# A decoder step with fp32 products from three passes: new orders and engine lists for the attention, the heads and the output projection

## The chip, the core and the metric

The kernel runs on one core of one Trainium2 chip. The core has a matmul engine (PE, with its weight loads shown as PEld), three engines for elementwise work (DVE, ACT and POOL) and SP, which here issues DMAs. The metric is the device time of one execution in microseconds (us), taken as the median of several runs; lower is better.

## The reference

It is one inference step of two layers over 512 prompt tokens and 8 single new tokens (520 columns together), width 1024, all in fp32. Layer 0 is native sparse attention with a paged cache, layer 1 an mLSTM with four heads of 512. Cut to what matters:

```python
x = x + (attend(rmsnorm(x) @ w_in) * silu(z)) @ w_out           # layer 0
# attend: gates[0]*compressed + gates[1]*selected + gates[2]*window, each a masked softmax over its keys
h = rmsnorm(x)                                                   # layer 1
xm, zm = split(h @ m_w_in)
c = silu(conv4(xm));  q, k, v = block4(c), block4(c), block4(xm)
C = decay * C + k (w v)^T                                        # 8 samples: state 4 x 512 x 512 each
S = (q k^T) * exp(D - m)                                         # prompt: one causal matrix for each head
hc = (S v) / max(|sum S|, exp(-m))                               # samples: q C + ... instead of S v
out = (hc * rsqrt(mean(hc^2)) * norm_w + skip * c) * silu(zm)
x = x + out @ m_w_out
y = rmsnorm(x)
```

The outputs are y, the new cache rows, and the new states C, n, m and conv.

## The kernel before

**Products.** An fp32 product is made of three fast passes. Every operand is split into a high part (`whi`, `hhi`, `uh`, `vh`, `kwh`, `Sh`) and the rest (`wlo`, `hlo`, `ul`, `vl`, `kwl`, `Sl`); `mm3` adds hi x hi, hi x lo and lo x hi in PSUM. A high part is a copy (by ACT or DVE), a low part a subtraction (by DVE or POOL). Some products run as plain fp32 (`s<-q,CT`, `mm<-CT,bdm`, `t<-bdk,ctw`), and those with the samples' state (`d<-cs,QZ`) use 32 columns of the array at a time, four side by side.

**Stages.** In time order: the input side of layer 0 (projection, compressed keys), the attention, then output projection, norm and the projection to xm with its convolution, then the gate side zm, then the heads of the mLSTM with most of its output projection, then a tail with the last head's output and the final norm. One weight tile passes through `wraw` (from HBM), `whi` and `wlo`.

**Order.** The program's text is not issued as it stands. Two recorders hold it back and replay it in an order written out by hand as a table of numbers. `Plan` holds named operations (a piece of work on one engine with what it reads and writes) and replays them at `P.run(ORDER0, R, NE, MOVEDP0)` (L1625, the attention), `P.run(ORDER1, ...)` (L2308, zm) and `P.run(ORDER2, R, NE, MOVEDP2)` (L2705, the heads). `Rec` holds every single instruction and replays at `R.run(NE, CALLS0, ...)` (L1024), `CALLS2` (L1415), `CALLS1, MOVED1` (L1952: output projection, norm, xm) and `CALLS3` (L2756, the tail). Each engine runs its own queue strictly in the order of issue; between engines semaphores hold back what needs another's result or buffer. Buffers come from pools that go round in the order of issue.

A number that also stands in a `MOVED` list changes engine when it is replayed:

```python
def swapped(engines, e, m, a, k):                        # L478
    if m == "activation":                                # a copy by ACT goes to DVE
        engines["DVE"].tensor_copy(a[0], a[1])
    elif m == "tensor_copy" and e == "DVE":              # a copy by DVE goes to ACT
        engines["ACT"].activation(a[0], a[1], AF.Copy)
    else:                                                # sub, mul, add, scalar: DVE <-> POOL
        getattr(engines["POOL" if e == "DVE" else "DVE"], m)(*a, **k)
```

Since every instruction goes through `Engine.__getattr__.call` (L504), all records of the profile bear this one line, and operations are told apart by the names of their tiles.

**The heads.** For each head and each of its four blocks of 128 columns `qk` (L2339) does: `mm<-CT,bdm` (PE) and its copy `q`; `ctw` (DVE), `t<-bdk,ctw` (PE), `kwh` (a copy) and `kwl` (a subtraction) of it; `s<-q,CT` (PE), the scores; and twelve `mm<-vh,kwh`, `mm<-vl,kwh`, `mm<-vh,kwl`, the new state C of the prompt, copied out by `cpt`. `values` (L2440) multiplies scores by decays (`wt`), splits them into `Sh` and `Sl`, and forms `num`; `sq` and `acc` are squares and their sum for the norm; `hx` and `hy` the factor; then num x `hy`, + `CT`, x `zs`, and the split into `uh` and `ul`. `out_unit` (L2633) is one tile of the output projection: `wraw`, `whi`, `wlo`, `mm<-uh,whi` and so on, and `x` += `mm`. For the samples `state_step` (L2014) does one of 32 pairs of head and sample: the state `cs` in, `d<-cs,QZ` (PE; `QZ` is q with the other samples at zero), `t<-VB,OH` (PE, v spread over the partitions), `cs` scaled (ACT), `cs` += `t` x `wk` (DVE), and `cs` out. In the attention, `pt` is a copy of softmax weights, `dxo` and `dPS` belong to the samples, and `mn` is the softmax maximum.

Of the kernel before, what the change touches and what calls it, by code (L numbers as in the profile page):

```python
# [540 lines left out]
def step_kernel(ctx, tc, ap):  # L541
# [1082 lines left out]
    P.LAT, P.SELF = 0.24, 0.07  # L1624
    P.run(ORDER0, R, NE, MOVEDP0)  # L1625
    actx.close()
# [324 lines left out]
    xm_val(15)  # L1951
    R.run(NE, CALLS1, MOVED1)  # L1952
    mctx.close()
# [912 lines left out]
```

## Time and profile before

| | |
|---|---|
| median of 3 runs | 1042.33 us (1041.23 to 1043.42) |
| the profiled execution | 1037.7 us, span 1036.0 us, granted clock 0.998 |
| PE busy | 1012.9 us, 98% of the span |
| PEld | 909.0 us, 88% |
| DVE | 784.4 us, 76% |
| ACT | 532.7 us, 51% |
| POOL | 380.6 us, 37% |
| memory | read 145.89 MB, written 58.10 MB, 197 GB/s over the span |

The busy time of PE is that of records whose ends are modelled; matmuls overlap, so consecutive starts are closer than the records are long. In the rows of the timeline the first number is the start in us, the second the length; square brackets hold the engine's idle time before the row and who ended it; `x8` are that many instructions grouped.

### The profile page before, as it was taken

To read this page: it belongs to the slowest core of one execution; us is meant where nothing else is said; L and a number is where in the kernel's file an instruction comes from. 1 tells how busy PE (TensorE), PEld (TensorE's weight loads), DVE (VectorE), ACT (ScalarE), POOL (GpSimd) and SP (SyncE) were. 2 spreads that over 40 slices of the span, in tenths; PEclk is the share of its full clock that TensorE was granted. 3 is DMA by queue.
4 is the path that set the end of the run, shared out by engine and by line. 5 is a ranking of instruction groups with operands and counts; after the bars stand their busy time and mean duration, and the time that the engine had idled before them with its cause. 6 is when DMAs were issued, how large, how long until landed. Compare 5 with 4: busy or idle time off the path is not lost.

```text
span 1036.0 us, 24026 instructions
## 1 busy us (share of the span) xinstructions
PE 1012.9 (98%) x8743; PEld 909.0 (88%) x8743; DVE 784.4 (76%) x1879; ACT 532.7 (51%) x1228; POOL 380.6 (37%) x430
## 2 busy tenths in 40 slices
PE   7999999999999999999999999999999999999998
PEld 6989999899998888779999998898857678877987
DVE  7876764568568987775887786866677888989885
ACT  5253342533268877761444455656655665463543
POOL 1072433301246656362234433332323335434330
PEclk9999999999999999999999999999999999999999
DMA  7664453133335624547434642688789789898543
GB/s 251 200 199 143 152 163 121 50 117 118 113 100 159 188 84 123 164 144 255 144 110 166 209 144 73 245 277 304 276 269 358 256 273 316 284 338 287 190 137 113
DMA packets 124793, 197.19 MB, mean 190 GB/s; under 512 B 16118, under 2 KB 66167, under 8 KB 124419
## 3 DMA queue, kind: packets, MB, share of 16 engines
q1 hardware_dynamic: 118866, 186.37, 54.7%
q10 hardware_dynamic: 5808, 9.28, 2.5%
q8 instruction: 69, 1.13, 0.4%
q14 instruction: 50, 0.40, 0.1%
HBM read 145.89 MB, written 58.10 MB: 197 GB/s over the span
## 4 chain that ended last, share of the span: by engine, by line
PE 67%; DVE 5%; ACT 2%; POOL 1%; issue 0%; DMA 0%; ACTq 0%; DVEq 0%
PE mm L504 44%; PE s L504 9%; PE t L504 8%; PE d L504 6%; ACT s L504 1%; DVE num L504 1%; DVE s L504 1%; POOL s L504 0%; DMA wraw<-in_m_in 0%; DVE ul L504 0%; DVE x L504 0%; ACT pt L504 0%; DVE wlo L504 0%; DVE hx L504 0%; DVE sc L504 0%
## 5 line engine op out<-in xcount | busy, mean ns | idle before, releaser
L504 PE MATMUL mm<-hhi,whi 128*128 128x260 f32 (+1 forms) x952 | 273.1, 287 | 0.9 <-ACT hhi L504 0.9
L504 PE MATMUL mm<-hhi,wlo 128*128 128x260 f32 (+1 forms) x952 | 269.9, 283 | 2.1 <-POOL wlo L504 1.1
L504 PE MATMUL mm<-hlo,whi 128*128 128x260 f32 (+1 forms) x952 | 269.6, 283 | 0.0
L504 PEld LDWEIGHTS mm<-hhi,whi 128*128 128x128 f32 (+1 forms) x952 | 178.4, 187 | 5.6 <-issue 3.6
L504 PEld LDWEIGHTS mm<-hhi,wlo 128*128 128x128 f32 (+1 forms) x952 | 178.3, 187 | 2.8 <-DVE wlo L504 1.5
L504 PEld LDWEIGHTS mm<-hlo,whi 128*128 128x128 f32 (+1 forms) x952 | 178.1, 187 | 0.8 <-DVE hlo L504 0.2
L504 POOL TENSOR_TENSOR wlo<-wraw,whi 128x1024 fp32r<-128x1024 f32 (+2 forms) x49 | 94.5, 1931 | 177.1 <-DVE whi L504 118.1
L504 DVE SCALAR_TENSOR_TENSOR cs<-t,wk,cs 128x512 f32<-128x512 f32 x128 | 89.1, 743 | 13.0 <-ACT cs L504 11.3
L504 ACT ACTIVATE cs<-cs,SBC 128x1024 f32<-128x1024 f32 x64 | 71.6, 1144 | 33.8 <-PE d L504 31.2
L504 POOL TENSOR_SCALAR s<-s,sm 128x256 f32<-128x256 f32 (+3 forms) x69 | 70.1, 1026 | 38.6 <-DVE sm L504 20.2
L504 ACT ACTIVATE s<-s,mn 128x256 f32<-128x256 f32 (+3 forms) x128 | 70.6, 554 | 16.8 <-DVE mn L504 12.8
L504 PE MATMUL s<-phi,w1h 128*128 128x256 f32 (+1 forms) x256 | 77.1, 301 | 0.0
L504 PE MATMUL s<-plo,w1h 128*128 128x256 f32 (+1 forms) x256 | 74.7, 292 | 2.3 <-DVE plo L504 2.3
L504 PE MATMUL s<-phi,w1l 128*128 128x256 f32 (+1 forms) x256 | 74.1, 289 | 0.0
L504 DVE TENSOR_TENSOR wlo<-wraw,whi 128x1024 fp32r<-128x1024 f32 (+1 forms) x53 | 61.1, 1154 | 9.2 <-ACT whi L504 4.5
L504 ACT ACTIVATE whi<-wraw 128x1024 fp32r<-128x1024 f32 (+1 forms) x53 | 46.7, 884 | 38.8 <-DMA wraw<-in_m_out 14.1
L504 PE MATMUL mm<-uh,whi 128*128 128x260 f32 x224 | 65.1, 291 | 0.0
L504 PE MATMUL mm<-uh,wlo 128*128 128x260 f32 x224 | 63.3, 282 | 1.5 <-DVE wlo L504 1.5
L504 DVE CUSTOM_DVE_ANT_0 s<-s,D 128x512 f32<-128x512 f32 (+3 forms) x128 | 57.8, 488 | 7.8 <-PE s L504 7.4
L504 PE MATMUL mm<-ul,whi 128*128 128x260 f32 x224 | 63.2, 282 | 0.0
L504 PEld LDWEIGHTS s<-plo,w1h 128*128 128x128 f32 x256 | 48.4, 189 | 4.0 <-DVE plo L504 2.8
L504 PEld LDWEIGHTS s<-phi,w1h 128*128 128x128 f32 x256 | 48.3, 189 | 0.6
(481 smaller groups left out, 2623.4 us busy)
## 6 DMA issues: line engine op xcount, KB each, us to landing
cs<-in_state_C SPq DMA_DIRECT2D x64, 512.0 KB, 6.5
o_cs<-cs SPq DMA_DIRECT2D x64, 512.0 KB, 5.0
praw<-in_cache SPq DMA_DIRECT2D x128, 128.0 KB, 3.0
dk<-in_cache SPq DMA_DIRECT2D x128, 128.0 KB, 2.6
wraw<-in_m_in SPq DMA_DIRECT2D x32, 512.0 KB, 4.0
wraw<-in_m_out SPq DMA_DIRECT2D x32, 256.0 KB, 4.9
wraw<-in_w_kv SPq DMA_DIRECT2D x11, 512.0 KB, 3.7
wraw<-in_w_q SPq DMA_DIRECT2D x8, 512.0 KB, 3.8
```

Source lines behind the costliest of these rows:

```text
L504: return f(*[real(x) for x in a], **{n: real(x) for n, x in k.items()})
```

## The change

Three tables of order are stated anew: `ORDER0` (934 numbers), `ORDER2` (933) and `CALLS1` (712); each is a permutation of the same numbers, with nearly all at another place (in the mean 10, 15 and 24 places away, at most 106, 135 and 251). With them go the lists of what changes engine: `MOVEDP0` from 118 to 123 numbers (41 new, 36 gone), `MOVED1` from 139 to 136 (62 new, 65 gone), `MOVEDP2` from 116 to 94 (44 new, 66 gone). `ORDER1`, `CALLS0`, `CALLS2`, `CALLS3` and their lists, all pools and all functions stay. PE and SP get the same instructions in another order; DVE has 20 instructions fewer, in the attention 392 and then 391, in the projection 268 and 245, in the heads 445 and 449 (ACT 244 and 247, 176 and 185, 230 and 239; POOL 104 and 102, 80 and 94, 101 and 88).

```diff
 ORDER0 = (
-    828, 792, 54, 55, 57, 834, 830, 8, 9, 108, 10, 11, 13, 14, 12, 71, 15, 37, 28, 793, 16, 17, 59, 60, 34, 61,
+    911, 830, 828, 792, 54, 55, 8, 13, 9, 10, 834, 11, 12, 71, 14, 15, 16, 17, 37, 28, 31, 61, 59, 57, 793, 18,
...
-MOVEDP2 = (82, 94, 170, 177, 189, 265, 272, 284, 285, 286, 288, 292, 295, 309, 338, 346, 357, 362, 373, 387, 388, 389,
+MOVEDP2 = (75, 82, 265, 285, 301, 304, 309, 328, 331, 347, 352, 356, 357, 373, 377, 387, 388, 391, 396, 397, 400, 405,
```

DVE at the start of the heads. `HN` is the last piece of the sample gates, `VT` is v of the prompt, `QKS` q and k of the samples, `pr`, `wk` and `nT` small parts of the samples' state n. Before:

```order
L504 TENSOR_TENSOR HN<-nm,dn 128x32
L504 CAST vh<-VT_9863 128x512
L504 CAST vh<-VT_10476 128x512
L504 COPY QZ_10218<-QKS 128x8 x4
L504 COPY q<-mm 128x512
L504 TENSOR_TENSOR pr<-QKS 128x32
L504 TENSOR_TENSOR pr<-QKS,nT 128x32
L504 TENSOR_TENSOR wk<-QKS,SBC 128x32
```

After:

```order
L503 TENSOR_TENSOR HN<-nm,dn 128x32
L503 COPY QZ_9877<-QKS 128x8 x4
L503 TENSOR_TENSOR VB<-t,VB 8x512
L503 ISA ctw,cwn<-CT_9724,wb 128x512
L503 ISA cwn 128x1
L503 ISA ctw,cwn<-CT_9799,wb 128x512
```

The copies `QZ` now follow `HN` directly; the two casts `vh` and the copy `q` are no longer on this engine here, and the small parts come behind `VB` and two `ctw`.

PE at the start of the heads, from the first `t<-bdk,ctw` to the first product with `kwh`. Before:

```order
L504 MATMUL t<-bdk,ctw 128x128 x4
L504 MATMUL s<-q,CT_9898 128x512
L504 MATMUL s<-q,CT_9898 128x384
L504 MATMUL s<-q,CT_9898 128x256
L504 MATMUL s<-q,CT_9898 128x128
L504 MATMUL mm<-CT_10067,bdm 128x512
L504 MATMUL t<-bdk,ctw 128x128 x4
L504 MATMUL s<-q,CT_9950 128x512
L504 MATMUL s<-q,CT_9950 128x384
L504 MATMUL s<-q,CT_9950 128x256
L504 MATMUL s<-q,CT_9950 128x128
L504 MATMUL mm<-vh,kwh 128x512
```

After:

```order
L503 MATMUL t<-bdk,ctw 128x128 x4
L503 MATMUL mm<-CT_10034,bdm 128x512
L503 MATMUL t<-bdk,ctw 128x128 x4
L503 MATMUL t<-VB,OH 128x512
L503 MATMUL mm<-vh,kwh 128x512
L503 MATMUL mm<-vl,kwh 128x512
```

The two blocks of scores that stood between `t<-bdk,ctw` and the product now stand ahead of both.

DVE at the end of the heads, up to the last `wlo` of the stage. Before:

```order
L504 TENSOR_TENSOR x_13343<-x_13343,mm 128x260 x2
L504 TENSOR_TENSOR x_12924<-x_12924,mm 128x260
L504 TENSOR_TENSOR num<-num,hy 128x512
L504 SCALAR_TENSOR_TENSOR num<-CT_11135,par,num 128x512
L504 TENSOR_TENSOR num<-num,zs 128x512 x2
L504 TENSOR_TENSOR wlo<-wraw,whi 128x512
```

After:

```order
L503 TENSOR_TENSOR x_12816<-x_12816,mm 128x260
L503 TENSOR_TENSOR x_13200<-x_13200,mm 128x260 x2
L503 TENSOR_TENSOR num<-num,hy 128x512
L503 SCALAR_TENSOR_TENSOR num<-CT_11127,par,num 128x512
L503 TENSOR_TENSOR num<-num,zs 128x512 x2
L503 TENSOR_TENSOR wlo<-wraw,whi 128x512
```

The `wlo` stands behind the same operations on `num`; from `hx` to it there are six additions to `x`, where there were seven.

More of the change, by code (lines that the diff above doesn't have):

```diff
@@ L251 @@
 CALLS1 = (
[33 rows of a table removed]
-)
-MOVED1 = (20, 27, 29, 30, 36, 45, 52, 61, 62, 69, 71, 72, 73, 79, 88, 89, 95, 104, 112, 117, 126, 127, 152, 157, 164,
[6 rows of a table removed]
[33 rows of a table added]
+)
+MOVED1 = (27, 29, 30, 36, 45, 46, 59, 67, 68, 72, 73, 79, 88, 89, 95, 105, 117, 124, 126, 127, 147, 152, 157, 164,
[6 rows of a table added]
 MOVED2 = (8, 9, 28, 47, 66, 84, 103, 104, 122, 123, 141, 142, 161, 177, 179, 185, 210, 212, 227, 240, 242, 249, 268,
@@ L295 @@
 MOVED3 = (2, 12, 16, 23, 30, 31, 35, 42, 65, 69, 103, 120, 124, 136, 141,)
-MOVEDP0 = (19, 20, 23, 24, 41, 47, 64, 65, 66, 67, 69, 84, 93, 95, 99, 119, 120, 123, 164, 166, 167, 184, 186, 190,
[5 rows of a table removed]
+MOVEDP0 = (7, 19, 20, 23, 24, 41, 47, 50, 64, 66, 69, 84, 86, 89, 93, 95, 98, 99, 119, 120, 124, 164, 167, 184, 186,
[5 rows of a table added]
 MOVEDP1 = (7, 27, 31, 42, 46, 47, 61, 77, 82, 87, 91, 112, 117, 127, 132, 136, 162, 166, 167, 172, 177, 181, 182, 192,
     196, 197, 202, 211, 212, 248, 255,)
-MOVEDP2 = (82, 94, 170, 177, 189, 265, 272, 284, 285, 286, 288, 292, 295, 309, 338, 346, 357, 362, 373, 387, 388, 389,
[5 rows of a table removed]
+MOVEDP2 = (75, 82, 265, 285, 301, 304, 309, 328, 331, 347, 352, 356, 357, 373, 377, 387, 388, 391, 396, 397, 400, 405,
[4 rows of a table added]
 LATE = ((3, 1), (3, 2), (3, 3))
```

269 rows, old and new, of tables (CALLS1, MOVED1, MOVEDP0, MOVEDP2) are left out of this document.

## The prediction

> **What bounds the kernel now.** I read the page's head first, then the windows, one for each stage, then the waits inside the three stages that are stated anew, and the timeline at the longest waits.
>
> ```profile
> PE 1012.9 (98%) x8743; PEld 909.0 (88%) x8743; DVE 784.4 (76%) x1879; ACT 532.7 (51%) x1228; POOL 380.6 (37%) x430
> ```
>
> The matmul engine is busy for 98% of the span, so time can come only from its 23.1 us of idle, from waits too short to show as idle, and from the cost of its own order. The windows say where the idle lies. Their columns are the stretch, its length, and each engine's busy time; the stretches are the input side, the attention, the output projection with norm and xm, zm, the heads, and the tail.
>
> ```profile
> core 0: us, PE busy (x) PEld busy (x) DVE busy (x) ACT busy (x) POOL busy (x), PEclk, DMA share, GB/s
> 0.00:307.00 307.00, 294.00 (x2431) 286.98 (x2431) 208.33 (x428) 124.03 (x301) 90.47 (x95) 1.00 0.45 144
> 307.00:467.00 160.00, 159.01 (x1902) 132.19 (x1899) 131.81 (x517) 122.00 (x377) 92.14 (x107) 0.99 0.48 143
> 467.00:647.00 180.00, 179.81 (x1572) 175.91 (x1576) 133.36 (x277) 77.05 (x176) 64.57 (x80) 1.00 0.47 157
> 647.00:751.00 104.00, 101.70 (x858) 92.72 (x851) 73.77 (x134) 62.61 (x119) 33.23 (x40) 1.00 0.79 276
> 751.00:993.00 242.00, 239.74 (x1725) 186.03 (x1724) 208.63 (x457) 129.78 (x215) 90.38 (x101) 1.00 0.83 282
> 993.00:1036.00 43.00, 38.61 (x269) 35.14 (x268) 28.54 (x70) 17.20 (x40) 9.77 (x9) 1.00 0.34 111
> ```
>
> Length less PE busy gives 13.0, 1.0, 0.2, 2.3, 2.3 and 4.4 us. The three stages that change (second, third and fifth row) hold 1.0 + 0.2 + 2.3 = 3.4 us of idle in 582 us; the other 19.7 us lie where the order stays. The granted clock is 0.99 to 1.00, so no stage is slowed by it. The waits of PE, in these three windows in turn (total, times, longest):
>
> ```profile
> PE t L504 <- DVE dxo L504: 0.2, 1, 0.2
> PE t L504 <- ACT pt L504: 0.2, 1, 0.2
> PE s L504 <- DVE mn L504: 0.2, 1, 0.2
> PE d L504 <- ACT pt L504: 0.2, 1, 0.2
> ...
> PE t L504 <- DVE sr L504: 0.2, 1, 0.2
> ...
> PE mm L504 <- DVE wlo L504: 1.5, 1, 1.5
> PE d L504 <- DVE QZ L504: 0.4, 1, 0.4
> PE mm L504 <- POOL Sl L504: 0.2, 1, 0.2
> ```
>
> So there is one wait of 1.5 us and one of 0.4, both in the heads; everything else is 0.2. A matmul record lasts longer than the distance to the next start, so short waits vanish under it:
>
> ```profile
> 766.42 0.39 PE L504 MATMUL mm<-vl,kwh 128*128 128x512 f32 x1
> 766.65 0.39 PE L504 MATMUL mm<-vh,kwl 128*128 128x512 f32 x1
> ...
> 458.21 0.49 PE L504 MATMUL t<-cst,s 128*128 128x128 f32 x3
> 458.91 0.33 PE L504 MATMUL t<-cst,dxo 128*128 128x128 f32 x1 [0.22 <-DVE dxo L504]
> ```
>
> The first pair starts 0.23 us apart with records of 0.39: a wait up to 0.16 us is not shown. In the second pair the start is 0.16 us later than the idle of 0.22 says. Twelve starts in the attention and four in the heads are late by 0.14 to 0.44 us against the usual spacing; 0.16 hidden in each is an estimate of 2.6 us beside the 3.4 shown. All that could be won by waits is therefore near 6 us.
>
> **The change part by part.** PE issues the same matmuls before and after; nothing is removed or added on it. What can move is the waits, the number of switches between forms of matmul, and the load of DVE, ACT and POOL by the pieces that change engine.
>
> *The wait at the start of the heads.* PE, then DVE and ACT:
>
> ```profile
> 754.47 1.99 PE L504 MATMUL d<-cs,QZ 128*32 128x512 f32 x16 [0.44 <-DVE QZ L504]
> 756.50 0.50 PE L504 MATMUL t<-VB,OH 128*128 128x512 f32 x1
> 756.83 2.32 PE L504 MATMUL s<-q,CT 128*128 128x512 f32 x8
> ...
> 753.43 0.75 DVE L504 CAST vh<-VT 128x512 fp32r<-128x512 f32 x2
> 754.10 0.38 DVE L504 COPY QZ<-QKS 128x8 f32<-128x8 f32 x4
> ...
> 755.66 2.19 ACT L504 ACTIVATE cs<-cs,SBC 128x1024 f32<-128x1024 f32 x2 [1.98 <-PE d L504]
> ```
>
> The QZ copies stand behind two casts that take 753.43 to 754.10. In the new order they stand first, so they end 0.67 us earlier, which is more than the 0.44 that PE waits: -0.44. The casts and a copy q that DVE had go to ACT, which idled 1.98 us there until PE gave cs free; a 512-column copy by ACT takes 0.63 (whi, next rows). PE's first s<-q,CT lies 756.83 - 754.47 = 2.4 us behind the start of d<-cs,QZ, so one more cast and the first q (1.3 us) are covered by ACT's idle time alone. Bounds: -0.44 to 0.
>
> *The wait at the end of the heads.* DVE, ACT and PE:
>
> ```profile
> 986.35 1.09 DVE L504 TENSOR_TENSOR x<-x,mm 128x260 f32<-128x260 f32 x3
> 987.35 0.69 DVE L504 TENSOR_TENSOR num<-num,hy 128x512 f32<-128x512 f32 x1
> ...
> 988.75 1.29 DVE L504 TENSOR_TENSOR num<-num,zs 128x512 f32<-128x512 f32 x2
> 989.95 0.68 DVE L504 TENSOR_TENSOR wlo<-wraw,whi 128x512 fp32r<-128x512 f32 x1
> ...
> 987.00 0.63 ACT L504 ACTIVATE whi<-wraw 128x512 fp32r<-128x512 f32 x1 [3.27 <-DMA wraw<-in_m_out]
> ...
> 990.69 0.39 PE L504 MATMUL mm<-uh,wlo 128*128 128x260 f32 x1 [1.55 <-DVE wlo L504]
> ```
>
> ACT's whi is there at 987.63, but wlo runs at 989.95 because num,hy / num,par / num,zs x2 stand ahead of it in DVE's queue. They stand there in the new order as well. Between hx and wlo one of seven additions to x is gone, 1.09 / 3 = 0.36 us, and DVE works there without a gap. So the wait shrinks from 1.55 to about 1.2: -0.36. Bounds: -1.55, if POOL's work no longer stretches DVE there (next point), and +1.1, if it stretches one operation more.
>
> *Sl.* Five POOL Sl go to DVE, which subtracts faster (a wlo of 512 columns 0.68 above, 1.70 on POOL below); the 0.2 wait for POOL's Sl goes, or another takes its place. I take -0.2; bounds -0.2 to +0.2.
>
> *Attention.* Four waits of 0.2, two of them on copies pt by ACT. Five pt of 512 go from DVE to ACT and three of 384 back, all orders are new; I find no place where a wait must go. I take half of the four, -0.4; bounds -1.0 (all idle there) and +1.0 (as many again).
>
> *Output projection, norm, xm.* DVE loses four whi and three wlo of 1024 columns and six bd of 128; ACT and POOL take them. By the rows of 512 columns (a cast 0.75 / 2 = 0.38, a subtraction 0.68) that is 4 x 0.76 + 3 x 1.36 + 6 x 0.17 = 8.1 of DVE's 133 us. PE idles 0.2 us there, so the relief has nothing to end: 0. Bounds -0.2 to +0.4 (two new waits of 0.2).
>
> *Switches on PE.* A 512-column matmul followed by one of its own kind starts 0.23 later, but t<-VB,OH at 756.50 is followed by s<-q,CT after 0.33: a switch costs 0.10. Counting neighbours of different kind in the order, the attention has 190 and then 192, the projection 42 and 44, the heads 83 and 86: +7, at most +0.7. The start of the heads, shown with the change, has fewer; in others a switch falls on a wait and costs nothing. I take +0.2; bounds -0.5 to +0.7. [...]
>
> *Engine load in the heads.* To DVE come five q, two cpt, two acc and three num,zs of 512 columns, 0.68 each by the row below, and five Sl of 1664 columns together (2.2): 10.4 us. From it go five vh and six whi at 0.38 and two kwh at 0.68: 5.5 us. DVE rises by about 4.9 from 208.6 of 242. What POOL does costs DVE as well:
>
> ```profile
> L504 DVE TENSOR_TENSOR num<-num,zs x8: 677/684/1780, 823.8 to 991.5; 128x512 f32<-128x512 f32 x8
> ...
> 981.32 1.70 POOL L504 TENSOR_TENSOR wlo<-wraw,whi 128x512 fp32r<-128x512 f32 x1 [5.95 <-ACT whi L504]
> ...
> 981.78 1.78 DVE L504 TENSOR_TENSOR num<-num,zs 128x512 f32<-128x512 f32 x1
> ```
>
> The longest num,zs, 1.78 instead of a median of 0.68, runs beside a POOL wlo: 1.1 us lost to DVE. Ten POOL operations fewer can give back up to 11 us, none if they lay beside other work; so DVE's net load is between +4.9 and -6.1. I cost it at nothing on PE: DVE had 33 us of slack there. If that cover goes, the returns in the third rival come late. [...]
>
> Sum: -0.44 - 0.36 - 0.2 - 0.4 + 0 + 0.2 = -1.2 us. The profiled execution took 1037.7 us, 1036.0 of it span, which is 4.6 below the median of 1042.33. I carry the difference over unchanged: 1042.3 - 1.2 = 1041.1. A difference under 0.2%, 2.1 us, can't be told from no change.
>
> **The rivals.**
>
> *Nothing goes* (time 1042.3). The waits have the size of one engine's operation, and a new order makes new ones of the same size. For it: sixteen places of 0.2 to 0.4 remain after an earlier tuning by the same kind of tables. Against it: QZ is first now, which no other part takes back.
>
> *Most waits go* (1038.0). Of the 6.0 us available, 70% vanish: -4.3. For it: every wait but one is under 0.5 us, and in the attention the matmuls between a score and the transposes that need its softmax come to 6.0 us at the shortest instead of 3.6, counted in the order with the starts' spacing. Against it: the end of the heads, a quarter of the sum, is the same in structure, and the work between transposes and products with V is as short as before. It decides for "faster" only if the 1.55 wait halves as well.
>
> *The returns in the heads come late* (1045.0). PE makes t<-bdk,ctw; ACT makes kwh of it, DVE kwl, and PE needs both:
>
> ```profile
> 759.23 1.05 PE L504 MATMUL t<-bdk,ctw 128*128 128x128 f32 x8
> 760.12 2.32 PE L504 MATMUL s<-q,CT 128*128 128x512 f32 x8
> 762.27 1.02 PE L504 MATMUL mm<-CT,bdm 128*128 128x512 f32 x2
> ...
> 766.10 0.48 PE L504 MATMUL mm<-vh,kwh 128*128 128x512 f32 x1
> ...
> 764.95 0.69 DVE L504 TENSOR_TENSOR kwl<-t,kwh 128x512 fp32r<-128x512 f32 x1
> ```
>
> Here PE has 766.10 - 760.12 = 6.0 us between the end of the first t<-bdk,ctw and the product. In the new order only one mm<-CT,bdm, the second t<-bdk,ctw and one t<-VB,OH stand between, at most 1.02 + 0.89 + 0.33 = 2.2 us, against 0.63 for kwh (a copy by ACT) and 0.69 for kwl in a row: 0.9 us of margin plus 2 x 0.23 until kwl is read. In the heads I count twelve such places with under 2 us of margin, where there were four. If DVE runs 1 us behind (one pair of cs or one stretched operation), each costs about 0.4, as the QZ wait did: 12 x 0.4 = 4.8, less the gains of 1.2 and a part that stays on time: about +2.7. It decides from seven late returns on. Against it: every place keeps some margin, and ACT and POOL are relieved or have room.
>
> **How the numbers follow.** The forecast, waits partly gone, 0.33; nothing goes, 0.14; most go, 0.31; returns late, 0.19; else 0.03, a DMA that comes later by the new order, on the slow side. The forecast's own range is 1039.5 to 1042.3 and reaches under -2.1 with 0.05 of its chance. Faster: 0.31 + 0.05 = 0.36; same: 0.28 + 0.14 = 0.42; slower: 0.22. For the range I take the bounds of the terms together with the rivals: low 1036.8 (waits gone and 1 us for the timing), high 1045.8.
>
> **What would show it.** In the new profile: PE idle in the heads near 1.5 us and no wait for QZ; the last wlo wait there near 1.2; the projection's idle still near 0.2 though its DVE time is about 8 us less; in the attention two or three waits of 0.2. Wrong it would be by a wait for kwl, q or VB in the heads that is not there now, by more than 1 us of change in the stages whose order stays, or by a wlo wait at the end over 2 us.

## The result and the profile after

The changed kernel takes 1049.87 us (median of 5 runs, 1049.27 to 1052.88), the kernel before 1042.53 in runs taken with it (5 runs, 1041.23 to 1044.59). The ratio is 1.0079, 95% interval 1.0059 to 1.0099: slower by about 7.3 us, where 1.2 us less had been forecast and the range ended at 1045.8.

The profiled execution of the changed kernel took 1049.27 us, its span is 1047.5 and its mean clock 0.993. The profiled execution of before lay at the lower end of that kernel's spread, so the spans differ by 11.5 us, more than the medians. The head of the page after, then its windows (attention, output projection with norm and xm, heads), with the columns as before:

```profile
PE 1018.2 (97%) x8743; PEld 912.9 (87%) x8743; DVE 787.3 (75%) x1859; ACT 542.9 (52%) x1249; POOL 383.6 (37%) x429
```

```profile
311.00:469.50 158.50, 157.13 (x1910) 130.95 (x1898) 134.03 (x515) 121.09 (x381) 93.14 (x105) 1.00 0.48 141
469.50:655.00 185.50, 182.16 (x1565) 177.28 (x1568) 125.71 (x256) 82.30 (x185) 74.87 (x94) 0.99 0.47 154
...
757.00:1004.00 247.00, 241.48 (x1727) 185.94 (x1728) 219.84 (x465) 134.94 (x224) 81.24 (x91) 0.99 0.82 278
```

PE's idle time rose from 23.1 to 29.3 us (span less PE busy): from 0.2 to 3.3 in the projection and from 2.3 to 5.5 in the heads. PE's busy time rose too, by 5.3 us, with the same 8743 matmuls, so part of the loss is a slower clock and not a wait: 0.998 less 0.993 is 5 us in 1047. The 6.2 of idle and the 5 of clock make up nearly all of the difference of the spans. Of the clock's part 3.4 us come from two half-clock stretches in a row (6.83 us at 0.50) at 205 us, in the input side, whose order stays (311 us in this execution, 307 before). Six of the 14 traces have half clock at that place, so this part can't be put down to the change.

The waits of PE in the three stages, in turn (total, times, longest):

```profile
PE d L503 <- ACT dpt L503: 0.8, 1, 0.8
PE mm L503 <- DVE pt L503: 0.3, 1, 0.3
...
PE d L503 <- ACT QKS L503: 1.7, 2, 1.2
PE mm L503 <- DVE xm L503: 1.0, 1, 1.0
PE d L503 <- POOL bd L503: 0.5, 1, 0.5
...
PE t L503 <- DVE pr L503: 2.1, 1, 2.1
PE mm L503 <- DVE kwl L503: 1.9, 1, 1.9
PE mm L503 <- DVE wlo L503: 1.6, 1, 1.6
PE t L503 <- DVE cwn L503: 0.9, 1, 0.9
```

The wait for `pr` is at the seam from zm to the heads and was there before. The waits for `dpt`, `QKS`, `xm`, `bd`, `kwl` and `cwn` are new. The wait for `QZ` is gone.

**Two new places in the projection.** `VS` and `QKS` are tiny copies of the samples' v, q and k out of the PSUM bank `d`, first `VS`, then `QKS`; PE needs the bank for the next `d<-CT,bd`. The timeline at the first place:

```profile
568.80 0.69 DVE L503 CAST whi<-wraw 128x1024 fp32r<-128x1024 f32 x1 [1.66 <-PE mm L503]
...
569.61 0.16 DVE L503 COPY VS<-d 128x8 f32<-128x8 f32 x1
...
569.87 0.18 ACT L503 ACTIVATE QKS<-d 128x16 f32<-128x16 f32 x1 [5.41 <-DVE VS L503]
...
570.10 0.61 PE L503 MATMUL d<-CT,bd 128*128 128x8 f32 x4 [1.21 <-ACT QKS L503]
```

DVE's next operation in the new order is a cast `whi`, which waits until PE gives up a weight buffer. `VS`, 0.16 us long, is queued behind it; ACT's `QKS` follows `VS`, and PE waits for `QKS`. So PE waits for a copy that waits for PE. In the tables before, `VS` and `QKS` of this block stand ahead of that `whi` (positions 294 and 304 against 338; now 322 and 323 against 319). The second place has the same pattern with ACT and DVE exchanged:

```profile
617.84 1.06 ACT L503 ACTIVATE whi<-wraw 128x1024 fp32r<-128x1024 f32 x1 [3.83 <-PE mm L503]
...
618.80 0.16 ACT L503 ACTIVATE VS<-d 128x8 f32<-128x8 f32 x1
...
618.99 0.17 DVE L503 COPY QKS<-d 128x16 f32<-128x16 f32 x1 [2.64 <-ACT VS L503]
...
619.31 0.58 PE L503 MATMUL d<-CT,bd 128*128 128x8 f32 x4 [0.50 <-POOL bd L503]
...
620.65 0.42 DVE L503 TENSOR_TENSOR xm<-mm,rr 128x260 f32<-128x260 f32 x1
...
621.12 0.39 PE L503 MATMUL mm<-hhi,whi 128*128 128x260 f32 x1 [1.00 <-DVE xm L503]
```

The profile puts the 0.50 down to POOL's `bd`, which ended at 619.29, just behind `QKS` (619.16). In the kernel with both places mended (below) the same `d<-CT,bd` starts at 616.79, ahead of that `bd` at 617.04, so `d` did not need it and `QKS` was what held PE. The `xm` is late because it stands behind `QKS` on DVE, which idled 2.64 us until ACT's `VS` was done.

**The clock behind the second place.** Windows of the changed kernel cut at 3.4 us; the number behind the five engines is the granted clock:

```profile
618.20:621.60 3.40, 1.90 (x16) 1.64 (x15) 2.61 (x6) 0.76 (x2) 0.83 (x2) 1.00 0.89 265
621.60:625.00 3.40, 3.40 (x18) 3.40 (x17) 1.58 (x5) 3.12 (x8) 0.00 (x0) 0.50 0.06 3
625.00:628.40 3.40, 3.40 (x31) 3.40 (x30) 3.33 (x6) 0.56 (x2) 2.88 (x4) 1.00 0.00 0
```

Behind the window with 1.5 us of idle the whole next one is at half clock here (0.50 from 621.60 to 625.00): 18 matmuls instead of 31, 1.7 us lost, as much as the waits themselves. The windows of before have this too, but not here (one at 387 us, in the attention).

**Two new places in the heads.** DVE, POOL and PE at the wait for `cwn`, then at the wait for `kwl`:

```profile
805.44 1.61 DVE L503 CUSTOM_DVE_ANT_0 ctw<-CT,wb 128x512 f32<-128x512 f32 x1
...
806.98 1.75 DVE L503 CUSTOM_DVE_ANT_0 ctw<-CT,wb 128x512 f32<-128x512 f32 x1
...
805.23 2.96 POOL L503 TENSOR_TENSOR acc<-acc,sq 128x512 f32<-128x512 f32 x2 [5.72 <-ACT sq L503]
...
808.80 1.16 PE L503 MATMUL t<-bdk,ctw 128*128 128x128 f32 x8 [0.87 <-DVE cwn L503]
...
903.31 1.51 DVE L503 CAST uh<-num 128x512 fp32r<-128x512 f32 x1
...
905.47 0.68 DVE L503 TENSOR_TENSOR kwl<-t,kwh 128x512 fp32r<-128x512 f32 x1
...
903.10 1.44 POOL L503 TENSOR_TENSOR ul<-num,uh 128x512 fp32r<-128x512 f32 x1 [0.26 <-ACT uh L503]
...
906.30 0.47 PE L503 MATMUL mm<-vh,kwh 128*128 128x512 f32 x1 [1.94 <-DVE kwl L503]
```

Beside a POOL operation with two inputs, `ctw` takes 1.61 and 1.75 us and the cast `uh` 1.51. What they take without it is shown by the kernel without POOL beside DVE, below.

### The profile page after: what moved, and what is told of

Same layout as the page of the kernel before. It is cut to its first block, busy times and chain, and to the rows that moved or that the text cites. A ratio compares the mean times of both kernels' runs of the same rounds, so it can differ in the third digit from the quotient of the medians.

```text
span 1047.5 us, 24056 instructions
## 1 busy us (share of the span) xinstructions
PE 1018.2 (97%) x8743; PEld 912.9 (87%) x8743; DVE 787.3 (75%) x1859; ACT 542.9 (52%) x1249; POOL 383.6 (37%) x429
## 4 chain that ended last, share of the span: by engine, by line
PE 65%; DVE 5%; ACT 2%; DMA 1%; issue 1%; POOL 1%; ACTq 0%; DVEq 0%; POOLq 0%; SPq 0%
PE mm L503 42%; PE s L503 10%; PE t L503 8%; PE d L503 6%; DMA cs<-in_state_C 1%; DVE num L503 1%; DVE s L503 1%; ACT s L503 1%; ACT pt L503 0%; DVE x L503 0%; POOL sacc L503 0%; DVE ul L503 0%; DVE ctw L503 0%; DMA o_cs<-cs 0%; POOL s L503 0%
## 5 line engine op out<-in xcount | busy, mean ns | idle before, releaser
L503 PEld LDWEIGHTS mm<-hhi,whi 128*128 128x128 f32 (+1 forms) x952 | 180.6, 190 | 7.7 <-issue 2.7
L503 PEld LDWEIGHTS mm<-hhi,wlo 128*128 128x128 f32 (+1 forms) x952 | 180.6, 190 | 2.5 <-POOL wlo L503 1.3
L503 PEld LDWEIGHTS mm<-hlo,whi 128*128 128x128 f32 (+1 forms) x952 | 180.5, 190 | 0.8 <-DVE hlo L503 0.2
L503 POOL TENSOR_TENSOR wlo<-wraw,whi 128x1024 fp32r<-128x1024 f32 (+2 forms) x51 | 99.9, 1960 | 209.1 <-DVE whi L503 95.9
L503 POOL TENSOR_SCALAR s<-s,sm 128x128 f32<-128x128 f32 (+3 forms) x67 | 69.9, 1052 | 43.1 <-DVE sm L503 17.1
L503 ACT ACTIVATE s<-s,mn 128x384 f32<-128x384 f32 (+3 forms) x128 | 70.8, 556 | 16.3 <-DVE mn L503 7.7
L503 ACT ACTIVATE whi<-wraw 128x1024 fp32r<-128x1024 f32 (+1 forms) x63 | 54.4, 869 | 45.5 <-PE mm L503 15.4
L503 DVE TENSOR_TENSOR wlo<-wraw,whi 128x1024 fp32r<-128x1024 f32 (+1 forms) x51 | 57.3, 1124 | 9.6 <-ACT whi L503 5.2
L503 DVE CUSTOM_DVE_ANT_0 s<-s,D 128x128 f32<-128x128 f32 (+3 forms) x128 | 56.7, 485 | 6.2 <-PE s L503 5.2
```

The costliest lines, as they stand in the source:

```text
L503: return f(*[real(x) for x in a], **{n: real(x) for n, x in k.items()})
```

## The experiments

The question was whether the loss is the projection's, by the order of `VS` and `QKS` against `whi`, or whether the heads' waits beside POOL carry as much. The recorded expectations give their theories letters; each says what its letters mean, and a letter can mean something else in another. Each kernel is the kernel before or the changed one with the numbers named moved. The line number that all records share differs from kernel to kernel and means nothing.

**Each stage alone.** The kernel before with the tables of one stage from the changed kernel.

```diff
-CALLS1, MOVED1      (of before)
+CALLS1, MOVED1      (of the changed kernel)
```

> The kernel before with only the projection's table and engine list (CALLS1, MOVED1) of the changed kernel; attention and heads as before. Theory A (the loss is new waits of PE on engines whose queue is held up): the trace after shows 3.3 us of idle in this stage where before had 0.2, so +3 us, or +3 to +6 if each wait also lowers the granted clock for a while. Rival B (the loss is spells of a lower granted clock that fall anywhere, whatever the order): no difference beyond 0.2%, and the clock of this kernel's runs like that of the kernel before on this chip. Rival C (the loss is on PE itself, switches between kinds of matmul): two switches more, at most +0.2 us.

Measured: 1048.74 us, ratio 1.0057 (1.0035 to 1.0078), clock 0.992 or 0.993 in all six runs. The waits of the changed kernel's projection stand there again, and so does the half-clock window:

```profile
619.90:623.30 3.40, 1.90 (x16) 1.65 (x15) 2.38 (x6) 0.99 (x2) 0.82 (x2) 1.00 0.93 282
623.30:626.70 3.40, 3.40 (x17) 3.40 (x17) 1.58 (x5) 2.89 (x8) 0.00 (x0) 0.50 0.08 4
```

So the projection is most of the loss: 6.3 us by the medians, 5.9 by the ratio, against 7.3 and 8.2 for the whole change. That is neither "no difference" (rival B) nor at most 0.2 us (rival C).

```diff
-ORDER2, MOVEDP2     (of before)
+ORDER2, MOVEDP2     (of the changed kernel)
```

> The kernel before with only the heads' table and engine list (ORDER2, MOVEDP2) of the changed kernel. Theory A: idle in this stage 4.6 us after (waits for cwn 0.9, kwl 1.9, wlo 1.6) where before had 2.3, so +2.3 us, up to +4 with a lower clock behind the waits; the wait for QZ is gone in it. Rival B: no difference beyond 0.2%. Rival C: three switches more, at most +0.3 us.

Measured: 1041.34 us, ratio 1.0006 (0.9986 to 1.0026). The waits are there (`cwn` 0.87, `kwl` 1.37, `wlo` 1.60 us), but the time can't be told from before. The interval still allows the 2.7 us by which the stage is longer in the trace.

```diff
-ORDER0, MOVEDP0     (of before)
+ORDER0, MOVEDP0     (of the changed kernel)
```

> The kernel before with only the attention's table and engine list (ORDER0, MOVEDP0) of the changed kernel. Theory A: idle in this stage 1.4 us after, 1.0 before, so +0.4 us, no difference that can be told. Rival B: the same, no difference. Rival C: two switches more, +0.2 us. If this part alone gives more than +2 us, all three are wrong here.

Measured: 1041.23 us, ratio 0.9991 (0.9976 to 1.0007): no change that can be told, though two waits (`dpt` 0.8, `pt` 0.3) replace the four of 0.2.

**The end of the heads.** The kernel before, with the last `wlo` of the stage on POOL.

```diff
-MOVEDP2 = (...)
+MOVEDP2 = (..., 917)
```

> The kernel before with one subtraction moved: the last wlo of the heads goes from DVE, where it stands behind three multiplications of num, to POOL, which idled 7.1 us there. The prediction took the wait of 1.55 us at this place as one engine's queue. If that is right, wlo is ready near 987.6 + 1.3 = 988.9 in the trace's time and the wait falls to 0.1 or less; the span falls by 0.5 to 1.5 us, less if the tail then waits for ul, which DVE makes from the same num. If POOL's work stretches DVE's multiplications there by 1.1 us, half of the gain is lost.

Measured: 1042.96 us, ratio 1.0002 (0.9981 to 1.0022). The wait of 1.55 for `wlo` is gone, and two came in its place right behind, 0.85 for POOL's `bdk` and 0.30 for POOL's `wlo`. The subtraction that was moved (992.93 to 994.28 on POOL) made DVE's work beside it longer: num,par at 993.16 took 1.67 us instead of 0.75. POOL's `bdk` waits for DVE's `num`. No gain.

**`VS` and `QKS` first.** The changed kernel with both copies put ahead of `whi` at both places (327 and 518 are `VS`, 326 and 517 `QKS`, 405 and 595 `whi`).

```diff
-    275, 404, 405, 286, 358, 327, 326, 222,
+    275, 404, 327, 326, 405, 286, 358, 222,
...
-    505, 595, 518, 517, 553,
+    505, 518, 517, 595, 553,
```

> The changed kernel with four copies moved in the projection: VS and QKS of two blocks stand ahead of a copy whi instead of behind it (one on DVE, one on ACT); all else as changed. Theory A: whi waits for PE to give a weight buffer free, VS behind it comes late, QKS waits for VS, and PE waits for the bank of PSUM or for xm behind QKS. Then the idle of 1.21 us (for QKS) and of 1.00 us (for xm) fall to under 0.3 each, and the spell of half clock that followed the second (1.71 us lost) goes: 2 to 4 us less than the changed kernel, 1046 to 1048. Rival B (spells of half clock are independent of the order): the waits go, -2 us, but the mean granted clock stays at 0.993. Rival D (the waits come from the order of PE itself, QKS is only the last to be seen): the waits stay within 0.3 us.

Measured: 1046.71 us, ratio 1.0044 (1.0024 to 1.0064). In its trace the waits of 1.2 and 1.0 us are gone, and no window near 621 us is at half clock; the waits left in the projection are:

```profile
PE mm L470 <- ACT VS L470: 0.7, 1, 0.7
PE d L470 <- ACT QKS L470: 0.4, 1, 0.4
PE t L470 <- DVE VT L470: 0.4, 1, 0.4
PE mm L470 <- DVE xm L470: 0.3, 1, 0.3
```

At the second place the order of the copies was the cause. In all, 3.2 us came back by the medians and 3.6 by the ratios, half of the loss or less. At the first place PE still waits. By the trace, the chain there is:

```profile
566.87 0.69 DVE L470 CAST whi<-wraw 128x1024 fp32r<-128x1024 f32 x1 [1.58 <-PE mm L470]
567.48 0.48 DVE L470 COPY VT<-t 128x128 f32<-128x128 f32 x2
567.80 0.28 ACT L470 ACTIVATE VT<-t 128x128 f32<-128x128 f32 x1 [2.23 <-DVE VT L470]
567.97 0.17 ACT L470 ACTIVATE VS<-d 128x8 f32<-128x8 f32 x1
568.20 0.39 PE L470 MATMUL mm<-hhi,whi 128*128 128x260 f32 x1 [0.68 <-ACT VS L470]
567.88 3.62 DVE L470 SCALAR_TENSOR_TENSOR cva<-xm,par,cva 128x510 f32<-128x510 f32 x2
```

`whi` still waits for PE, and now `VT` stands behind it; ACT's `VT` waits for DVE's, and the next block's `VS` stands behind that. So it is the same chain by one more copy. Then the two `cva`, 1.63 us in the changed kernel, take 3.62 beside POOL's `wlo` (567.78 to 570.17), and the next `VT` behind them is late. No kernel tests these two readings.

**The seam from zm to the heads.** The wait for `pr` is the longest near the heads in both kernels. In the kernel before, the samples' small chain that ends in `pr` goes ahead of the last product of zm, and in a second kernel the first `QZ` copy goes first in the heads as well.

```diff
 ORDER1 = (
-    207, 209, 218, 219,
+    207, 209, 336, 337, 338, 339, 247, 218, 219,
```

> The kernel before with five operations of the zm stage moved: the chain of the samples' norm (t<-sd,ncs to t<-cst,lse) is issued ahead of the last product of zm (24 matmuls, 2.9 us) instead of behind it. PE waited 2.05 us for pr there, in both kernels. Theory A (an idle stretch costs its length, and a spell of half clock behind it in some executions; it stood there in 2 of the 6 profiles): the wait falls under 0.3 us, -2 us, and the mean clock rises by about 0.0005: in all -2 to -3 us. Rival B: -2 us, clock unchanged. Rival D: the chain waits elsewhere (DVE's additions zt stand in its way), the gain is under 0.5 us.

```diff
 ORDER2 = (
-    22, 282, 290, 303, 284, 402, 291, 2, 3, 1,
+    22, 282, 290, 303, 1, 284, 402, 291, 2, 3,
```

> As the kernel with the samples' norm ahead of the last product of zm, and the copies QZ ahead of the casts vh at the start of the heads, as in the changed kernel. The step of the prediction on QZ: 0.44 us of wait gone there, so 0.4 us less than that kernel, 2.4 to 3.4 less than before. If DVE reaches QZ early in any case, since the chain ahead of it ends earlier, there is no difference between the two.

Measured: 1043.1 us (1.0011, 0.9992 to 1.0030) and 1044.22 us (1.0015, 0.9995 to 1.0035). Both missed. The wait for `pr` went and another came in its place, here in the first of the two:

```profile
PE mm L488 <- POOL bdm L488: 2.7, 1, 2.7
```

`bdm` stands on POOL behind an operation that needs the last product of zm; with the chain moved ahead, it became the last to arrive. The wait for `QZ` is in neither of the two traces, so the second kernel's own edit had nothing left to remove.

**Heads without POOL beside DVE.** The kernel before with the changed kernel's heads, but the two `acc` and the `ul` of the places shown moved from POOL to DVE.

```diff
 MOVEDP2      (of the changed kernel)
-    ..., 373, ..., 521, ...
+    ..., 369, ...
```

> The kernel before with only the heads changed, and three operations moved from POOL to DVE: two acc of the first head, which ran on POOL beside two ctw of DVE (1.61 and 1.75 us instead of 0.69), and one ul, which ran on POOL beside a cast uh of DVE (1.51 us instead of 0.42). Theory P (POOL and DVE hold each other up at the memory): DVE gets 2.1 us more work, yet ctw and uh take 0.7 and 0.4 us, PE's wait for cwn (0.87) falls under 0.2 and that for kwl (1.37 to 1.94) by 0.6 or more; 1 to 1.5 us less than with the heads alone. Rival L (only the load of DVE counts): ctw and uh keep their length or DVE is later by 0.7 at kwl, and the waits stay or grow.

Measured: 1043.5 us, ratio 1.0017 (0.9994 to 1.0040). DVE at the two places:

```profile
800.38 0.68 DVE L500 CUSTOM_DVE_ANT_0 ctw<-CT,wb 128x512 f32<-128x512 f32 x1
...
800.99 0.69 DVE L500 CUSTOM_DVE_ANT_0 ctw<-CT,wb 128x512 f32<-128x512 f32 x1
...
898.72 0.41 DVE L500 CAST uh<-num 128x512 fp32r<-128x512 f32 x1
```

Without POOL beside them the same operations take 0.68, 0.69 and 0.41 us instead of 1.61, 1.75 and 1.51, the wait for `cwn` is gone, and PE's wait at the product with `kwh` is 0.75, put down to ACT's `whi` (1.94 for `kwl` in the changed kernel, 1.37 in the heads alone, from which this kernel differs by the three operations). So the stretching made the one wait and about half of the other. Where the two engines hold each other up, at the memory (as theory P has it) or elsewhere, no run shows. The time did not fall: `t<-acc,ones` now waits 1.72 us, since the `acc` came later in DVE's queue.

**One place at a time.** The edit of the kernel with `VS` and `QKS` first, at the second place alone, and at the first alone.

```diff
-    505, 595, 518, 517, 553,
+    505, 518, 517, 595, 553,
```

> The changed kernel with VS and QKS put back ahead of the weight copy whi at the second place of the projection alone (619 us); the first place (570 us) as changed. Theory A (two places that add up; the second costs 1.0 us of wait and nearly always a half-clock window of 1.7 us behind it): about 2.2 to 2.7 us below the changed kernel, 1047.0 to 1048.2, no half-clock window between 615 and 630 us in the profile, the 1.21 us wait at 570 still there. Rival R (the window belongs to the idle of both places together, or to something else): the window at 621 us stays and the gain is at most the 1.0 us of wait, 1049 or more.

```diff
-    275, 404, 405, 286, 358, 327, 326, 222,
+    275, 404, 327, 326, 405, 286, 358, 222,
```

> The changed kernel with VS and QKS put back ahead of the weight copy at the first place (570 us) alone; the second place as changed. Theory A: the 1.21 us wait shrinks to 0.7 or less, the 1.0 us wait at 619 and the half-clock window behind it stay; 0.5 to 1.2 us below the changed kernel, 1048.5 to 1049.8, clock still about 0.993. Rival R: this place alone gives back 2 us or more (under 1048).

Measured: 1046.56 us for the second place (ratio to before 1.0035, 1.0017 to 1.0053), 3.3 below the changed kernel by the medians and 4.6 by the ratios (the two were not run together), and 1050.42 for the first (1.0074, 1.0050 to 1.0098), no gain. The second gave more than the 2.2 to 2.7 expected, the first less than the 0.5 to 1.2. All that the kernel with both places mended gave back is the second place's; with it mended, 3.5 us of the loss remain against before in the same runs. The mean clock follows the place: 0.9930, 0.9925 and 0.9930 in the changed kernel, the projection alone and the first place alone, which leave the second as it is, against 0.9952 and 0.9954 where it is mended and 0.9949 to 0.9962 in the groups of runs of the kernel before. The difference of about 0.0024 is 2.5 us of 1047; a half-clock window costs 1.7 / 1047 = 0.0016, so it is about one and a half windows an execution. The second place can account for one of them; what the rest is stays open. Of the four traces that leave this place as changed, three have the half clock behind it; in the fourth, with the longer wait below, its 1.5 us of idle lay across a boundary of the windows (0.57 and 0.93).

At the first place, where the fix took 1.21 us away, waits of 0.7 and 0.4 came instead, for `VS` and `VT`. The first place can bring half clock too: in the profiled execution with only the second mended, the wait of 1.21 us was followed by it.

```profile
568.30:571.70 3.40, 2.19 (x20) 1.98 (x18) 1.97 (x6) 0.42 (x3) 0.24 (x1) 1.00 0.02 5
571.70:575.10 3.40, 3.40 (x18) 3.40 (x18) 0.91 (x2) 1.27 (x2) 3.22 (x3) 0.51 0.00 0
```

The same wait had none behind it in the two other traces that have it.

**A longer wait.** The changed kernel with `VS` and `QKS` of the first place behind the pair of `cva` (364, 365).

```diff
-    358, 327, 326, 222, 284, 364, 365, 287,
+    358, 222, 284, 364, 365, 327, 326, 287,
```

> The changed kernel with VS and QKS at the first place put behind two more DVE operations (the pair of cva, 1.63 us): the wait of PE grows from 1.21 to about 2.8 us. Theory C (a grid of 3.41 us windows; a window with 2.0 us or more of idle makes the next one run at half clock): 2.8 us of idle puts 2.0 into one window in about 8 of 10 positions of the grid, so besides the 1.6 us of wait most executions lose another 1.7: 1.6 + 1.4 = 3.0 us above the changed kernel, 1052 to 1053.5, mean clock near 0.9917, and a half-clock window at 571 to 577 us in the profile unless the boundary lies in the middle of the wait. Rival I (idle costs only its own length): 1051 to 1051.7, clock unchanged at 0.993.

Measured: 1052.57 us (1.0097, 1.0075 to 1.0120), 2.7 above the changed kernel by the medians and 1.9 by the ratios, with a mean clock of 0.9930 over six runs, as in that kernel (theory C expected 0.9917). By the medians the time lies in the range that was stated for C, by the ratios between the two theories; the clock speaks for I. With six runs it stays open. In its profiled execution no window behind the wait is at half clock, though it is 2.86 us long:

```profile
566.40:569.80 3.40, 1.70 (x15) 1.48 (x13) 1.75 (x5) 0.28 (x1) 0.00 (x0) 1.00 0.02 5
569.80:573.20 3.40, 2.25 (x19) 2.25 (x20) 1.02 (x3) 1.41 (x4) 1.77 (x2) 1.00 0.00 0
573.20:576.60 3.40, 3.40 (x32) 3.40 (x31) 1.10 (x3) 0.66 (x1) 1.27 (x2) 1.00 0.03 2
```

The wait lies across a boundary of the grid on which that execution's half-clock windows lie, so each window has under 2 us of idle: the exception that was named, but no proof.

**Everything but the projection.** The changed kernel with the projection's tables of before.

```diff
-CALLS1, MOVED1      (of the changed kernel)
+CALLS1, MOVED1      (of before)
```

> The changed kernel with the order of the output projection, norm and xm from before; attention and heads as changed. Theory A (the loss is the projection's): the losses go, the attention keeps about 0.4 of gain and the heads cost up to 1.5; 1040.5 to 1043.0, not to be told from before. Rival S (the parts work on each other, since buffers and clock windows carry over): 1044.5 or more.

Measured: 1043.24 us, ratio 1.0004 (0.9988 to 1.0020). With the projection's order back, the loss is gone; attention and heads together are worth nothing that can be told. No kernel tried is faster than before beyond its interval.

## Why the prediction was wrong

**Output projection: 0, bounds -0.2 to +0.4. This step failed.** It was measured at +5.9 to +6.3 us by itself. I summed what DVE loses in work (its busy time did fall, from 133.4 to 125.7) and said that relief has nothing to end there; I did not follow the order on DVE and ACT, which for this table is the largest part of the change. Compared in the profiled executions from the first `mm<-uo,whi` to the `d<-cs,QZ` at the stage's end, less 1.7 for the half-clock window, the stage is 4.2 us longer (466.86 to 646.75 is 179.9; 469.46 to 655.27, less 1.7, is 184.1). Four late starts carry 3.8 of it (1.38, 0.61, 0.66 and 1.15 beyond the usual spacing: `QKS` twice, `bd`, `xm`). With the window's 1.7 that makes 5.9. With both places mended the stage is still 3.3 us longer than before; four late starts carry 2.4 of it (against the usual spacing 0.82 for `VS`, 0.58 for `VT`, 0.61 for `QKS` and 0.43 for `xm`). The 0.61 stands in the changed kernel as well, at 585.45, and nothing was tried on it: ACT's `QKS` stands behind copies that wait for a DVE `cva`, 1.68 us instead of 0.75 beside POOL's `CT`. So about half of the loss is shown by edits to come from the second place; for the rest the stage is shown, and the places are read from traces alone.

**"The granted clock is 0.99 to 1.00, so no stage is slowed by it": this step failed too.** 0.99 over 160 us is one window of 3.4 us at half clock. I took a rounding for an absence, and carried the 4.6 us between the profiled execution and the median over as a constant. Over all runs the time goes with the mean clock, about 1 us for each 0.001 (a fit with one level for each kernel), and the kernel before moves by itself between clocks of 0.992 and 1.000. Its 18 runs at 0.998, the clock of the profiled execution, took 1039.5 us in the mean, so some 2.9 of the 4.6 us are half-clock windows that this execution happened not to have; the rest stays open. By the mean clock, a change in the waits went with a change in the number of such windows: 0.9925 to 0.9930 where the second place is as changed, 0.9952 and 0.9954 where it is mended.

**Start of the heads, -0.44: right in the trace.** No wait for `QZ` is left; no timed kernel shows a gain from it. **`Sl`, -0.2: right**, it is gone.

**End of the heads, -0.36: missed.** The wait for `wlo` is 1.61 where 1.2 was forecast. The addition that left gave 0.36 less work, but POOL's `wlo` at 996.06 now lies beside a num,par at 996.44, which takes 1.67 us instead of 0.75. Before, the POOL `wlo` at 983.80 lay beside a num,hy, which took 1.15 instead of 0.69. So DVE lost 0.92 there instead of 0.46, a little more than the 0.36 that it won. It is the mechanism of the upper bound ("if it stretches one operation more"), by another operation in place of one. In the kernel without POOL beside DVE the only wait left at the end of the stage is 0.24.

**Attention, -0.4: not told apart.** Its idle rose from 1.0 to 1.4 us; timed alone it came out 0.9991, with 0.9976 to 1.0007.

**Switches, +0.2: right in size.** With the usual spacing of each pair of neighbours, the sums differ by -0.2 in the projection and +0.4 in the heads. For the attention the sum depends on which rare pairs are counted (+0.1 to +0.6), so this is an estimate.

**Engine load in the heads, 0: missed, and the rival half right.** DVE's busy time there rose by 11.2 us (208.6 to 219.8), where the prediction allowed from -6.1 to +4.9. Fewer POOL operations did not mean fewer beside DVE: at two places POOL's `acc` and `ul` lie beside `ctw` and `uh`, and the returns `cwn` and `kwl` came 0.9 and 1.9 us late. The rival "returns late" named `kwl` and DVE running behind, but for the place where the order leaves the least margin (the start of the heads), where no wait came. Margin in the order told little here; what lay beside POOL told more. The stage is 2.7 us longer in the trace, and nothing could be told in the timed runs.

**Two small slips.** 70% of 6.0 us is 4.2 and not 4.3, and the low end of the range comes out at 1037.0 from the terms named, not 1036.8. Neither bears on the result.

**The range** ended at 1045.8 because every bound was a wait of one or two operations. None allowed a chain in which a short copy stands behind a long one that waits for PE itself, and none a price for idle beyond its length.

## What to carry over

When an order is changed, follow each short copy that gives PE its next PSUM bank: if on its engine it stands behind an operation that waits for PE (a cast into a weight buffer that PE still reads), PE waits for itself, however idle that engine is (1.21 us at the first place, with DVE idle for 1.66). Look at every copy behind that operation and not only at the first: where one was moved ahead here, the next took its place. For a kernel like this one, look at the idle of a whole 3.41 us window and not at each wait alone: where it came to 1.97 us or more, a half-clock window followed in all 13 cases of these traces, at a cost of 1.7 us, and with less one sometimes did. And read engine load by what lies beside what: one POOL operation with two inputs at the wrong moment cost DVE about 1 us here (`ctw` 1.61 and 1.75 instead of 0.69, `uh` 1.51 instead of 0.41), and with ten fewer in the stage as a whole its busy time still rose by 11.2.

## What the runs showed of the hardware

**Half-clock windows.** In all 14 traces the clock, on record from 11.6 to 14.8 us into the span, is either full or 0.50, the latter in stretches of 3.41 us (or twice that), whose starts within one execution differ by multiples of 3.413 us (in the changed kernel 205.19, 621.61 and 758.15, 122 and 40 such lengths apart); the grid lies differently in each execution. Cut on that grid, from the first clock record to PE's last matmul, all 13 windows with 1.97 us or more of PE idle (up to 2.31) were followed by one at half clock, and one of 12 with 1.70 to 1.91. Some windows with less idle were followed by one too, and held tiny matmuls: 1.50 us of idle with the 8-column `d<-CT,bd` (the second place, in the three traces where that wait lay whole in one window), and none at all with `d<-VNEW,dpt`, which uses 8 rows by 32 columns of the array, as in the kernel before:

```profile
384.20 1.93 PE L504 MATMUL d<-VNEW,dpt 8*32 8x256 f32 x32
```

```profile
383.70:387.10 3.40, 3.40 (x52) 2.23 (x52) 2.99 (x13) 1.92 (x9) 2.35 (x4) 1.00 0.02 5
387.10:390.50 3.40, 3.40 (x15) 3.00 (x14) 2.83 (x11) 2.88 (x11) 2.03 (x3) 0.50 0.00 0
```

This place was followed by half clock in 11 of 14 traces; in five of these the order is the new one, with the wait of 0.8 for `dpt` inside the window. In two of the other three the group lay across a boundary; in the third (the first kernel of the seam) it lay whole in one window and full clock followed, which stays unexplained. Four more half-clock windows followed 1.61, 1.43, 1.21 and 0.19 us of idle, with small matmuls in the window each time, and three followed a window that was at half clock itself. The grid goes a long way to explain why one kernel's runs spread over several us: the wait of 2.05 us for `pr` cost 1.7 more where it fell whole into one window, as it did in 5 of the traces. In the changed kernel 754.70 to 758.10 has 2.05 us of idle and the next window is at 0.51; in the kernel before the wait lies across a boundary, 748.90 to 752.30 has 1.75, and the next is at 1.00. What sets off a half-clock window, idle time or small matmuls or both, was not settled; the kernel with the longer wait did not do it.

**DVE beside POOL.** A two-input POOL operation made `ctw` 2.3 to 2.5 times as long (0.69 to 1.61 and 1.75 us) and even a copy with one input 3.7 times (`uh`, 0.41 to 1.51).
